# Sample attention of a hybrid decoder: four pages of values in four column groups, and scores of two sequences to a step

## The chip, the cores and the metric

The kernel runs on one NeuronCore of a Trainium2 chip. Its engines are TensorE (matmuls; PE in the rows, its weight loads PEld), VectorE (DVE), ScalarE (ACT), GpSimd (POOL) and SyncE (SP), each with an instruction queue of its own that it works off in order; 16 DMA engines move data between HBM and SBUF. The metric is the device time of one execution in microseconds (us); the time of a kernel is the median of its runs.

## The reference

One inference step of a two-layer decoder, for a prompt of 512 tokens and a group of 8 samples with one new token each. Each layer is a half-step FFN, a mixer and a half-step FFN. The first layer's mixer joins differential attention (4 heads, two softmax maps each) with gated linear attention (GLA); the second's is an mLSTM. The change lies in the attention of the 8 samples, over 2048 cached keys and values each, in 16 pages of 128 positions that a page table points to:

```python
def diff_weights(logits, lam):
    p = jax.nn.softmax(logits, axis=-1)
    return p[:, :, 0] - lam * p[:, :, 1]

def diff_attn_sample(q, k_new, v_new, k_past, v_past, lam, slopes):
    ...
    logits = jnp.concatenate([
        alibi_logits(q, k_past, q_pos, jnp.arange(past), slopes),
        alibi_logits(q, k_new, q_pos, q_pos, slopes)], axis=-1)
    w = diff_weights(logits, lam)
    return (jnp.einsum('bhqk,bkhv->bqhv', w[..., :past], v_past.astype(F32))
            + jnp.einsum('bhqk,bkhv->bqhv', w[..., past:], v_new.astype(F32)))
...
        k_past = cache_k[e, page_table].reshape(dec_b, past, H_A, 2, DK_A)
        v_past = cache_v[e, page_table].reshape(dec_b, past, H_A, DV_A)
        a_out = diff_attn_sample(aq, ak, av, k_past, v_past, lam, slopes)
```

The new token attends to the past and to itself; per sequence, head and map there is one row of 2048 scores, and per sequence and head one row of 128 values comes out. Everything is fp32.

## The kernel before

The program is one straight row of stages: FFN, the even mixer (`even`), two FFNs, the odd mixer, FFN. Dense products are split into a high and a low half (fp32r operands; three matmuls at lines 100 to 102), and their weights come through `raw`, which in the even mixer is fetched over GpSimd's queue.

The even mixer computes, in this order, queries and keys of the prompt (tiles `pj`, the projections), values, prompt attention (`aps`, `atp`, `ao`), then GLA for two pairs of heads (`gla_pair`: masked products `glv`, decays `gdc`, state updates `gu`, outputs `go`; `gla_sample`: `gsu`, `gso`), then the output projection (`project`, tile `y`). Four more projections (`gates`, tile `pj`) are dealt out over the first GLA pair; the second has none.

The attention of the samples is a generator, `sample_steps`, that is advanced between other work: `tick(us)` adds the time of the work just written down and advances the queue by one step for each `rate` (1.65 us) of it; the projection's `rest` empties what is left (`tick(1e9)`). The generator writes:

- Scores (line 730, tile `sps`). A unit is two pages of keys (512 KB, `kv_unit`, two DMAs from SP's queue, four buffers of tile `kv`). For each of 8 groups `u` of two pages and each of 8 sequences `b`, four matmuls, one per head, with 32 stationary columns in column group `h` (`tile_position=(0, 32 * h)`), stream 256 key positions. One sequence to a step.
- Softmax over [128 rows = 4 heads x 32, 2048] (`sc`, `sm`, `m1`), and 16 transposes (`stp`) that turn the weights so that positions lie on partitions.
- Values (line 776, tile `so`). For each `b`, each group `g` of four pages and each page `i`, four matmuls, one per head in its column group, stream the 128 value columns of that head. The stationary `pw` is zero but for the two columns of the sequence (line 771 copies them in, line 768 clears the old ones on GpSimd, after the matmuls that read them). One unit of two pages to a step, 8 matmuls.
- The end (lines 783 to 790): scale by `w`, one matmul with `sel` that turns and sums the rows, one for the new token, and two adds into `oa`.

Instructions are not run in the order in which the code writes them. A scheduler puts them on each engine's queue by priority (work within `tc.high_priority` first) and by when its model of the machine has their operands ready; so a step's matmuls can be apart on TensorE, with other matmuls between them. An fp32 matmul shows as two passes in the profile (each a weight load and a matmul), a transpose and an fp32r matmul as one.

Of the kernel before, what the change touches and what calls it, by code (L numbers as in the profile page):

```python
# [7 lines left out]
F32 = mybir.dt.float32  # L8
# [3 lines left out]
ALU = mybir.AluOpType  # L12
# [3 lines left out]
P = 128  # L16
# [3 lines left out]
NS = 8  # L20
# [9 lines left out]
KU, PTU, KVB, PLAG = 2, 2, 4, 8  # L30
# [25 lines left out]
class Net:  # L56
# [663 lines left out]
    def sample_steps(self):  # L720

        nc, ev = self.nc, self.ev
        mx = self.smx
        sc = []
        for u in range(16 // KU):
            ps = self.plong.tile([P, 512], F32, tag="long", name="sps")
            for b in range(NS):
                kt = self.kv_unit(self.t["ckt"], "kt")
                for h in range(4):
                    nc.tensor.matmul(ps[32 * h:32 * h + 32, :KU * P], lhsT=self.q2[:, b, h, :],  # L730
                                     rhs=kt[:, :, h * P:h * P + P], start=(b == 0), stop=(b == NS - 1),
                                     tile_position=(0, 32 * h))
                if b < NS - 1:
                    yield True
            if u % 2 == 0:
                sc.append(ev.tile([P, 512], F32, tag="sc", name="sc", bufs=SCB))
            r = slice(KU * P * (u % 2), KU * P * (u % 2 + 1))
            nc.vector.tensor_tensor_reduce(out=sc[-1][:, r], in0=ps[:, :KU * P], in1=self.sbias[:, r], scale=1.0,
                                           scalar=-3e38, op0=ALU.add, op1=ALU.max, accum_out=mx[:, u:u + 1])
            yield True  # L740
        sm, nb, m1 = [ev.tile([P, 9], F32, tag=f"sm{i}", name="ssm") for i in range(3)]
        off = self.sbias[:, 512:521]
        nc.vector.tensor_tensor(out=nb, in0=mx, in1=off, op=ALU.add)
        nc.vector.tensor_reduce(out=m1[:, 0:1], in_=nb, axis=AX.X, op=ALU.max)
        nc.vector.tensor_scalar(nb, off, m1[:, 0:1], None, ALU.subtract)
        for g in range(4):
            nc.scalar.activation(sc[g], sc[g], AF.Exp, bias=nb[:, 2 * g:2 * g + 1], accum_out=sm[:, g:g + 1])
        nc.scalar.activation(sm[:, 4:5], mx[:, 8:9], AF.Exp, bias=nb[:, 8:9])
        nc.vector.tensor_reduce(out=m1[:, 1:2], in_=sm[:, :5], axis=AX.X, op=ALU.add)
        nc.vector.reciprocal(m1[:, 2:3], m1[:, 1:2])  # L750
        w = m1[:, 3:4]
        nc.vector.tensor_tensor(out=w, in0=self.rw, in1=m1[:, 2:3], op=ALU.mult)
        nc.vector.tensor_tensor(out=self.wnew, in0=sm[:, 4:5], in1=w, op=ALU.mult)
        yield True
        tps = []
        for g in range(4):
            tp = self.bank("stp")
            for i in range(4):
                nc.tensor.transpose(tp[:, i * P:i * P + P], sc[g][:, i * P:i * P + P], self.ident)
            s = ev.tile([P, 512], F32, tag="sc", name="spt", bufs=SCB)  # L760
            self.evict(s, tp)
            tps.append(s.rearrange("p (i h x) -> p i h x", i=4, h=4))
            yield True
        o = self.plong.tile([P, 512], F32, tag="long", name="so")
        for b in range(NS):
            if b:
                for a in self.pw:
                    nc.gpsimd.memset(a[:, :, :, 2 * b - 2:2 * b], 0.0)
            for g in range(4):
                pw = self.pw[g % 2]  # L770
                nc.vector.tensor_copy(pw[:, :, :, 2 * b:2 * b + 2], tps[g][:, :, :, 2 * b:2 * b + 2])
                for i in range(4):
                    if i % KU == 0:
                        vt = self.kv_unit(self.t["cv"], "vtile")
                    for h in range(4):
                        nc.tensor.matmul(o[32 * h:32 * h + 32, :P], lhsT=pw[:, i, h, :],  # L776
                                         rhs=vt[:, i % KU, h * P:h * P + P], start=(b == 0 and g == 0 and i == 0),
                                         stop=(b == NS - 1 and g == 3 and i == 3), tile_position=(0, 32 * h))
                    if i % KU == KU - 1 and not (b == NS - 1 and g == 3 and i == 3):
                        yield True  # L780

        ob = self.vtile()[:, :P]
        nc.vector.tensor_scalar(ob, o[:, :P], w, None, ALU.mult)
        yield True
        f = self.bank("sf")
        nc.tensor.matmul(f[:, :32], lhsT=ob, rhs=self.sel, start=True, stop=True)
        nc.tensor.matmul(f[:, 32:64], lhsT=self.wnew.to_broadcast([P, P]), rhs=self.sel, start=True, stop=True)
        z = self.oa[:, :, SEQ:]
        nc.vector.tensor_tensor(out=z, in0=f[:, 32:64].rearrange("p (h b) -> p h b", h=4), in1=self.vs, op=ALU.mult)
        nc.vector.tensor_tensor(out=z, in0=f[:, :32].rearrange("p (h b) -> p h b", h=4), in1=z, op=ALU.add)  # L790

    def attn_weights(self, i, h):
        nc, at = self.nc, self.at
# [237 lines left out]
    def even(self, w_in, w_out):  # L1031
        from contextlib import ExitStack
        nc, tc, t = self.nc, self.tc, self.t
        with ExitStack() as ctx:
# [3 lines left out]
            def const(name, shape, dt=F32, pool=None):  # L1038
                a = (pool or ev).tile(shape, dt, tag=name, name=name)
                nc.gpsimd.dma_start(out=a, in_=t[name])  # L1040
                return a
# [8 lines left out]
            bhn = const("bhn", [P, 4])  # L1050
            self.sbias = const("sbias", [P, 521])
            self.sel = const("sel", [P, 32])
            rm = const("rmask", [P, 2])
            lt = ev.tile([P, 2], F32, tag="lt", name="lt")
            self.nlam = ev.tile([P, 1], F32, tag="nlam", name="nlam")
# [16 lines left out]
            self.vs = ev.tile([P, 4, NS], F32, tag="vs", name="vs")  # L1072
            self.qs = ev.tile([P, 4, NS], F32, tag="qs", name="qs")
            oa = self.oa = ev.tile([P, 4, T], F32, tag="oa", name="oa")
            self.pw = [ev.tile([P, 4, 4, 32], F32, tag=f"pw{i}", name="pw") for i in range(2)]
            self.q2 = ev.tile([P, NS, 4, 32], F32, tag="q2", name="q2")
            for a in self.pw + [self.q2]:
                nc.gpsimd.memset(a, 0.0)
# [19 lines left out]
            with ExitStack() as c2:  # L1098
# [60 lines left out]
                ob = self.ob = gl.tile([P, 4, T], F32, tag="ob", name="ob")  # L1159
# [536 lines left out]
def even_consts():  # L1696
    f = np.float32
    c = {}
    p = np.arange(P)
    half, sel, rm = np.zeros((P, 32), f), np.zeros((P, 32), f), np.zeros((P, 2), f)  # L1700
    half[:64, 0], half[64:, 1] = 1, 1
    slope = SLOPE
    sb = np.zeros((P, 521), f)
    for h, b, m in itertools.product(range(4), range(NS), range(2)):
            r = 32 * h + 2 * b + m
            sb[r, :512] = [-slope[h] * (512 - c_) for c_ in range(512)]
            sb[r, 512:520] = [-slope[h] * (2048 - 512 * (g // 2 + 1)) for g in range(8)]
            rm[r, m] = 1
            sel[r, 8 * h + b] = 1
    c["half"], c["sbias"], c["rmask"], c["sel"] = half, sb, rm, sel  # L1710
    dist = 384 + p[:, None] - np.arange(512)[None, :]
    c["dist"] = np.where(dist >= 0, -dist, -1e30).astype(f)
    lvl = np.zeros((P, 9, P), f)
    msk = np.zeros((P, 8, P), np.int32)
    a, b = p[:, None], p[None, :]
    for lv in range(7):
        w = 64 >> lv
        mid = b // (2 * w) * (2 * w) + w
        lvl[:, lv, :] = np.where(b >= mid, (a >= mid) & (a <= b), (a > b) & (a < mid)) / 16.0
        msk[:, lv, :] = (a // (2 * w) == b // (2 * w)) & (a % (2 * w) < w) & (b % (2 * w) >= w)  # L1720
    lvl[:, 7, :] = (a <= b) / 16.0
    lvl[:, 8, :] = (a > b) / 16.0
    msk[:, 7, :] = a == b
    c["lvl"], c["gmask"] = lvl.reshape(P, 9 * P), msk
    return c
# [119 lines left out]
```

## Time and profile before

| | before |
|---|---|
| median of 3 runs | 2262.44 us (2254.84 to 2271.28) |
| the profiled execution | 2272.11 us, its span 2270.3 us |
| TensorE busy | 2224.2 us (98%), 18340 matmuls |
| VectorE, ScalarE, GpSimd busy | 1513.6 (67%), 1010.9 (45%), 47.5 us (2%) |
| mean granted clock of TensorE | 0.977 |
| HBM read, written | 276.22 MB, 17.11 MB |
| `kt<-ckt`, `vtile<-cv` | 128 issues each, 256 KB each, 4.3 and 3.7 us to landing |

A row of the profile names line, engine, operation, and tiles as out<-in, with the operand's partitions x elements; busy times are those that the profiler records, so in a pipelined row of matmuls the recorded ends overlap the next start, and the distance from start to start is what a matmul takes. The granted clock is the share of 2.4 GHz that TensorE's throttle let through (1.00 or 0.50; other figures are means over a stretch). The even mixer lies between about 340 and 835 us, the sample scores between 428 and 584, the sample values between 596 and 801.

### The profile page before, as it was taken

To read this page: it belongs to the slowest core of one execution; us is meant where nothing else is said; L and a number is where in the kernel's file an instruction comes from. 1 tells how busy PE (TensorE), PEld (TensorE's weight loads), DVE (VectorE), ACT (ScalarE), POOL (GpSimd) and SP (SyncE) were. 2 spreads that over 40 slices of the span, in tenths; PEclk is the share of its full clock that TensorE was granted. 3 is DMA by queue.
4 is the path that set the end of the run, shared out by engine and by line. 5 is a ranking of instruction groups with operands and counts; after the bars stand their busy time and mean duration, and the time that the engine had idled before them with its cause. 6 is when DMAs were issued, how large, how long until landed. Compare 5 with 4: busy or idle time off the path is not lost.

```text
span 2270.3 us, 45692 instructions
## 1 busy us (share of the span) xinstructions
PE 2224.2 (98%) x18340; PEld 2082.8 (92%) x18340; DVE 1513.6 (67%) x3161; ACT 1010.9 (45%) x1932; POOL 47.5 (2%) x112
## 2 busy tenths in 40 slices
PE   8999999999999999999999999999999999999999
PEld 8999998776776689999999999999889899999999
DVE  8858586435664478676768758586745588858683
ACT  6535354335522255344444535353545555525352
POOL 0000001000000000000000000000000000000000
PEclk9999999999996699999999999999999999999999
DMA  5324234587775552323223324232554464233322
GB/s 179 110 66 133 67 111 134 177 275 249 246 233 168 169 186 66 121 85 112 84 85 112 112 67 129 73 102 75 140 154 145 149 205 141 93 103 94 103 84 85
DMA packets 107019, 296.30 MB, mean 131 GB/s; under 512 B 12129, under 2 KB 16786, under 8 KB 106678
## 3 DMA queue, kind: packets, MB, share of 16 engines
q1 hardware_dynamic: 93504, 254.91, 35.3%
q0 software_dynamic: 7536, 25.42, 3.6%
q10 hardware_dynamic: 5766, 13.05, 1.6%
q8 instruction: 144, 2.36, 0.4%
q14 instruction: 69, 0.57, 0.1%
HBM read 276.22 MB, written 17.11 MB: 129 GB/s over the span
## 4 chain that ended last, share of the span: by engine, by line
PE 84%; DVE 6%; DMA 6%; ACT 2%; issue 2%; SPq 0%; POOL 0%; ACTq 0%; POOLq 0%; DVEq 0%
PE y L100 9%; PE y L101 8%; PE y L102 8%; PE A L100 6%; PE A L101 6%; PE A L102 6%; PE pj L100 3%; PE pj L101 3%; PE pj L102 3%; PE E L101 3%; PE E L100 3%; PE E L102 3%; DMA cs<-sc 2%; PE glv L899 2%; PE so L776 2%
## 5 line engine op out<-in xcount | busy, mean ns | idle before, releaser
L105 ACT CAST whi<-raw 128x512 fp32r<-128x512 f32 (+1 forms) x440 | 351.2, 806 | 435.0 <-PE y L101 171.3
L106 DVE TENSOR_TENSOR wlo<-raw,whi 128x512 fp32r<-128x512 f32 (+1 forms) x440 | 402.0, 922 | 156.4 <-ACT whi L105 142.5
L100 PE MATMUL y<-hh,whi 128*128 128x256 f32 (+1 forms) x1408 | 398.1, 283 | 0.0
L101 PE MATMUL y<-hl,whi 128*128 128x256 f32 (+1 forms) x1408 | 397.9, 283 | 0.0
L102 PE MATMUL y<-hh,wlo 128*128 128x256 f32 (+1 forms) x1408 | 396.8, 282 | 0.0
L100 PE MATMUL pj<-xh,whi 128*128 128x264 f32 (+1 forms) x896 | 263.8, 295 | 16.1 <-ACT gs L1531 3.2
L101 PEld LDWEIGHTS y<-hl,whi 128*128 128x128 f32 x1408 | 265.1, 188 | 1.0 <-DVE hl L106 0.6
L100 PEld LDWEIGHTS y<-hh,whi 128*128 128x128 f32 x1408 | 264.7, 188 | 0.8
L102 PEld LDWEIGHTS y<-hh,wlo 128*128 128x128 f32 x1408 | 264.8, 188 | 0.0
L102 PE MATMUL pj<-xh,wlo 128*128 128x264 f32 (+1 forms) x896 | 257.4, 288 | 2.9 <-DVE wlo L106 2.9
L101 PE MATMUL pj<-xl,whi 128*128 128x264 f32 (+1 forms) x896 | 258.6, 289 | 0.0
L100 PE MATMUL A<-xb,whi 128*128 128x264 f32 (+1 forms) x864 | 249.3, 290 | 0.7
L101 PE MATMUL A<-xb,whi 128*128 128x264 f32 (+1 forms) x864 | 244.2, 284 | 0.0
L102 PE MATMUL A<-xb,wlo 128*128 128x264 f32 (+1 forms) x864 | 243.0, 284 | 0.1
L105 ACT CAST whi<-graw 128x1024 fp32r<-128x1024 f32 x144 | 147.6, 1049 | 162.5 <-PE y L101 103.9
L100 PEld LDWEIGHTS pj<-xh,whi 128*128 128x128 f32 x896 | 173.1, 193 | 33.1 <-issue 10.3
L549 DVE SCALAR_TENSOR_TENSOR x<-y,x 128x256 f32<-128x256 f32 (+1 forms) x192 | 81.9, 427 | 180.5 <-PE y L102 180.1
L106 DVE TENSOR_TENSOR wlo<-graw,whi 128x1024 fp32r<-128x1024 f32 x144 | 172.6, 1219 | 30.9 <-ACT whi L105 30.9
L102 PEld LDWEIGHTS pj<-xh,wlo 128*128 128x128 f32 x896 | 172.9, 193 | 5.0 <-DVE wlo L106 3.3
L101 PEld LDWEIGHTS pj<-xl,whi 128*128 128x128 f32 x896 | 173.2, 193 | 4.0 <-issue 3.5
L100 PEld LDWEIGHTS A<-xb,whi 128*128 128x128 f32 x864 | 162.5, 188 | 9.2 <-DVE c L476 2.6
L100 PE MATMUL E<-xh,whi 128*128 128x264 f32 x576 | 163.7, 284 | 1.6 <-ACT whi L105 1.6
(468 smaller groups left out, 5179.9 us busy)
## 6 DMA issues: line engine op xcount, KB each, us to landing
raw<-w SPq DMA_DIRECT2D x240, 512.0 KB, 3.6
graw<-w SPq DMA_DIRECT2D x72, 512.0 KB, 4.4
kt<-ckt SPq DMA_DIRECT2D x128, 256.0 KB, 4.3
vtile<-cv SPq DMA_DIRECT2D x128, 256.0 KB, 3.7
raw<-w POOLq DMA_DIRECT2D x40, 512.0 KB, 4.5
cs<-sc SPq DMA_DIRECT2D x16, 512.0 KB, 6.9
kb<-kqd SPq DMA_DIRECT2D x16, 512.0 KB, 6.9
o_cs<-cs ACTq DMA_DIRECT2D x16, 512.0 KB, 5.3
```

Of the source, the lines that this page charges most:

```text
L100: nc.tensor.matmul(ps, lhsT=wh, rhs=xh, start=(ends[0] and i == ks[0]), stop=False, skip_group_check=open_)
L101: nc.tensor.matmul(ps, lhsT=wh, rhs=xl, start=False, stop=False, skip_group_check=open_)
L102: nc.tensor.matmul(ps, lhsT=wl, rhs=xh, start=False, stop=(ends[1] and i == ks[-1]), skip_group_check=open_)
L105: self.nc.scalar.copy(out=hi, in_=src)
L106: self.nc.vector.tensor_tensor(out=lo, in0=src, in1=hi, op=ALU.subtract)
L549: nc.vector.scalar_tensor_tensor(xs, y[:, :n], -0.5, xs, ALU.mult, ALU.add)
L776: nc.tensor.matmul(o[32 * h:32 * h + 32, :P], lhsT=pw[:, i, h, :], rhs=vt[:, i % KU, h * P:h * P + P], start=(b == 0 and g == 0 and i == 0 ...
L899: nc.tensor.matmul(ps[:, j * P:j * P + P], lhsT=lhs[r, j * P:j * P + P], rhs=rhs[r, j * P:j * P + P], start=True, stop=True)
```

## The change

Scores: the step takes two sequences. The first unit of keys is requested, a step ends, the second is requested, and then come the eight matmuls of both. The number of steps is the same.

Values: the roles are turned. The four pages `i` of a group now go to the four column groups, and each matmul streams the whole row of 512 values (four heads of 128). The 32 stationary columns hold four sequences x 4 heads x 2 maps (`pw` is [128, 4, 32]), so the work runs in two halves `hf` of four sequences each, each with its own `so` bank; per sequence and group of pages there are four matmuls after both units were requested, 128 in all. Rows of `so` mean page group, sequence, head and map, so that the weight per row is brought into that order by two matmuls with `perm` (`sw`, `wr`), and each half ends with a scaling of 512 columns and four matmuls with `sel2` (`sf`, `fs`) that sum over the page groups.

```diff
-            for b in range(NS):
-                kt = self.kv_unit(self.t["ckt"], "kt")
-                for h in range(4):
-                    nc.tensor.matmul(ps[32 * h:32 * h + 32, :KU * P], lhsT=self.q2[:, b, h, :],
-                                     rhs=kt[:, :, h * P:h * P + P], start=(b == 0), stop=(b == NS - 1),
-                                     tile_position=(0, 32 * h))
-                if b < NS - 1:
+            for b in range(0, NS, 2):
+                kts = [self.kv_unit(self.t["ckt"], "kt")]
+                yield True
+                kts.append(self.kv_unit(self.t["ckt"], "kt"))
+                for i, kt in enumerate(kts):
+                    for h in range(4):
+                        nc.tensor.matmul(ps[32 * h:32 * h + 32, :KU * P], lhsT=self.q2[:, b + i, h, :],
+                                         rhs=kt[:, :, h * P:h * P + P], start=(b + i == 0), stop=(b + i == NS - 1),
+                                         tile_position=(0, 32 * h))
+                if b < NS - 2:
                     yield True
...
+        f = self.bank("sw")
+        for hf in range(2):
+            nc.tensor.matmul(f[:, hf:hf + 1], lhsT=self.perm[:, hf * P:hf * P + P], rhs=w, start=True, stop=True)
+        wr = ev.tile([P, 2], F32, tag="wr", name="wr")
+        fs = ev.tile([P, 4, NS], F32, tag="fs", name="fs")
+        nc.vector.tensor_copy(wr, f[:, :2])
...
-        o = self.plong.tile([P, 512], F32, tag="long", name="so")
-        for b in range(NS):
-            if b:
-                for a in self.pw:
-                    nc.gpsimd.memset(a[:, :, :, 2 * b - 2:2 * b], 0.0)
-            for g in range(4):
-                pw = self.pw[g % 2]
-                nc.vector.tensor_copy(pw[:, :, :, 2 * b:2 * b + 2], tps[g][:, :, :, 2 * b:2 * b + 2])
-                for i in range(4):
-                    if i % KU == 0:
-                        vt = self.kv_unit(self.t["cv"], "vtile")
-                    for h in range(4):
-                        nc.tensor.matmul(o[32 * h:32 * h + 32, :P], lhsT=pw[:, i, h, :],
-                                         rhs=vt[:, i % KU, h * P:h * P + P], start=(b == 0 and g == 0 and i == 0),
-                                         stop=(b == NS - 1 and g == 3 and i == 3), tile_position=(0, 32 * h))
-                    if i % KU == KU - 1 and not (b == NS - 1 and g == 3 and i == 3):
+        for hf in range(2):
+            o = self.plong.tile([P, 512], F32, tag="long", name="so")
+            for b in range(4):
+                if hf or b:
+                    old = slice(8 * ((b + 3) % 4), 8 * ((b + 3) % 4) + 8)
+                    for a in self.pw:
+                        nc.gpsimd.memset(a[:, :, old], 0.0)
+                for g in range(4):
+                    pw = self.pw[g % 2]
+                    x = 8 * hf + 2 * b
+                    nc.vector.tensor_copy(pw[:, :, 8 * b:8 * b + 8].rearrange("p i (h m) -> p i h m", h=4),
+                                          tps[g][:, :, :, x:x + 2])
+                    vts = [self.kv_unit(self.t["cv"], "vtile")]
+                    yield True
+                    vts.append(self.kv_unit(self.t["cv"], "vtile"))
+                    for i in range(4):
+                        nc.tensor.matmul(o[32 * i:32 * i + 32, :], lhsT=pw[:, i, :], rhs=vts[i // KU][:, i % KU, :],
+                                         start=(b == 0 and g == 0), stop=(b == 3 and g == 3), tile_position=(0, 32 * i))
+                    if b < 3 or g < 3:
                         yield True
...
+            ob = self.vtile()[:, :512]
+            nc.vector.tensor_scalar(ob, o, wr[:, hf:hf + 1], None, ALU.mult)
+            yield True
+            f = self.bank("sf")
+            for h in range(4):
+                nc.tensor.matmul(f[:, 4 * h:4 * h + 4], lhsT=ob[:, h * P:h * P + P], rhs=self.sel2[:, 4 * h:4 * h + 4],
+                                 start=True, stop=True)
+            nc.vector.tensor_copy(fs[:, :, 4 * hf:4 * hf + 4], f[:, :16].rearrange("p (h b) -> p h b", h=4))
...
-            self.pw = [ev.tile([P, 4, 4, 32], F32, tag=f"pw{i}", name="pw") for i in range(2)]
+            self.pw = [ev.tile([P, 4, 32], F32, tag=f"pw{i}", name="pw") for i in range(2)]
```

The left-out lines load the two new constants (`sel2`, `perm`) and add `fs` into `oa`.

The order of instructions on the engines follows. Its rows give line, operation, tiles, and shape of the output; "x4" is four alike in a row. The first place is TensorE's queue in the second GLA pair, at its first state update `gsu`; `so` is the sample values, `glv`, `gso`, `gsu` and `gsot` belong to GLA. Before:

```order
L776 MATMUL so<-vtile,pw 32x128 x8
L1011 MATMUL gsu<-vt,ks 64x512 x2
L899 MATMUL glv<-gkq 128x128 x4
L776 MATMUL so<-vtile,pw 32x128 x8
L1021 MATMUL gso<-gst,qm 32x128 x4
L899 MATMUL glv<-gkq 128x128 x4
L776 MATMUL so<-vtile,pw 32x128 x8
L1027 MATMUL gsot<-ident,vt 128x128
```

The same place on TensorE's queue after the change:

```order
L917 MATMUL glv<-gkq 128x128 x4
L1029 MATMUL gsu<-vt,ks 64x512
L790 MATMUL so<-vtile,pw 32x512 x2
L1029 MATMUL gsu<-vt,ks 64x512
L917 MATMUL glv<-gkq 128x128 x3
L790 MATMUL so<-vtile,pw 32x512
L917 MATMUL glv<-gkq 128x128
L1039 MATMUL gso<-gst,qm 32x128 x3
L917 MATMUL glv<-gkq 128x128
L790 MATMUL so<-vtile,pw 32x512
```

Before, the eight matmuls of a step stood together; now the four of a step stand apart, as two, one and one, with GLA's matmuls between them, which are themselves cut.

The second place is TensorE's queue in the output projection, in the last steps of the sample values; `y` is the projection, `hst` and `hs` the statistics of a norm. Before:

```order
L224 MATMUL hst<-ident,row 128x128
L776 MATMUL so<-vtile,pw 32x128 x4
L224 MATMUL hst<-ident,row 128x128 x2
L101 MATMUL y<-xl,whi 128x256
L102 MATMUL y<-xh,wlo 128x256
L776 MATMUL so<-vtile,pw 32x128 x4
L100 MATMUL y<-xh,whi 128x256
```

The same place on TensorE's queue after the change:

```order
L102 MATMUL y<-xh,wlo 128x256
L790 MATMUL so<-vtile,pw 32x512 x2
L214 MATMUL hs<-sq,one 32x256
L790 MATMUL so<-vtile,pw 32x512
L224 MATMUL hst<-ident,row 128x128 x2
L100 MATMUL y<-xh,whi 128x256
L101 MATMUL y<-xl,whi 128x256
L102 MATMUL y<-xh,wlo 128x256
L100 MATMUL y<-xh,whi 128x256
L790 MATMUL so<-vtile,pw 32x512
```

Here too a group of four column groups was whole before; now it is three entries of the row. In the whole program `so` stands in 84 runs on TensorE before (36 of four matmuls, 25 of eight, 15 longer or of five to nine, 8 of fewer than four), and in 77 after (46 of one, 17 of two, 8 of three, 6 of four); `sps` in 51 before and 42 after.

## Rows read from the trace of the kernel before

**Rows 1.** The page, parts 1, 2 and 4: busy time, granted clock, chain.

```profile
PE 2224.2 (98%) x18340; PEld 2082.8 (92%) x18340; DVE 1513.6 (67%) x3161; ACT 1010.9 (45%) x1932; POOL 47.5 (2%) x112
...
PEclk9999999999996699999999999999999999999999
...
PE 84%; DVE 6%; DMA 6%; ACT 2%; issue 2%; SPq 0%; POOL 0%; ACTq 0%; POOLq 0%; DVEq 0%
```

**Rows 2.** Busy by stretch: length, PE, PEld, DVE, ACT, POOL; clock, DMA share, GB/s.

```profile
428.00:596.00 168.00, 165.31 (x1476) 119.77 (x1474) 75.90 (x279) 73.38 (x182) 10.33 (x20) 1.00 0.77 256
596.00:701.00 105.00, 104.59 (x1217) 81.56 (x1216) 68.35 (x165) 32.71 (x89) 7.34 (x23) 0.98 0.75 246
702.00:776.00 74.00, 74.00 (x441) 47.49 (x433) 24.37 (x73) 9.31 (x24) 1.85 (x6) 0.50 0.39 125
```

**Rows 3.** The same stretches, matmuls and weight loads of tile `so` alone.

```profile
596.00:701.00 105.00, 28.53 (x640) 16.50 (x640) 0.00 (x0) 0.98 0.75 246
702.00:776.00 74.00, 20.25 (x236) 7.00 (x228) 0.00 (x0) 0.50 0.39 125
776.00:802.00 26.00, 7.17 (x152) 3.08 (x144) 0.34 (x1) 1.00 0.84 282
```

**Rows 4.** What TensorE waited for, 428 to 802: total us, times, longest.

```profile
PE sps L730 <- DMA kt<-ckt: 1.3, 2, 0.8
PE so L776 <- DMA vtile<-cv: 0.5, 1, 0.5
```

**Rows 5.** Timeline of TensorE at full clock (start us, recorded us, matmul, count).

```profile
664.89 0.64 PE L776 MATMUL so<-vtile,pw 128*32 128x128 f32 x16
665.47 1.16 PE L899 MATMUL glv<-gkq 64*128 64x128 f32 x8
...
692.09 0.41 PE L776 MATMUL so<-vtile,pw 128*32 128x128 f32 x2
692.43 1.09 PE L934 MATMUL gu<-bv,gkn 128*64 128x128 f32 x16
...
785.25 0.28 PE L101 MATMUL y<-xl,whi 128*128 128x256 f32 x1
785.37 0.28 PE L102 MATMUL y<-xh,wlo 128*128 128x256 f32 x1
785.58 0.43 PE L776 MATMUL so<-vtile,pw 128*32 128x128 f32 x8
785.93 0.39 PE L101 MATMUL y<-xl,whi 128*128 128x256 f32 x1
```

**Rows 6.** The same view: a 512-wide fp32 matmul at full clock, and its follower.

```profile
640.22 1.07 PE L1011 MATMUL gsu<-vt,ks 8*64 8x512 f32 x2
641.22 0.64 PE L776 MATMUL so<-vtile,pw 128*32 128x128 f32 x14
```

**Rows 7.** The same view at half clock.

```profile
708.96 1.96 PE L1011 MATMUL gsu<-vt,ks 8*64 8x512 f32 x2
710.85 0.66 PE L776 MATMUL so<-vtile,pw 128*32 128x128 f32 x8
711.44 1.96 PE L1011 MATMUL gsu<-vt,ks 8*64 8x512 f32 x2
...
750.11 0.41 PE L101 MATMUL y<-xl,whi 128*128 128x256 f32 x1
750.32 0.41 PE L102 MATMUL y<-xh,wlo 128*128 128x256 f32 x1
```

**Rows 8.** Busy time by stretch: a short spell at half clock.

```profile
640.00:643.00 3.00, 3.00 (x26) 1.06 (x21) 1.42 (x6) 0.00 (x0) 0.00 (x0) 1.00 0.71 211
643.00:647.00 4.00, 4.00 (x20) 3.72 (x20) 2.09 (x13) 0.00 (x0) 0.00 (x0) 0.57 0.73 254
```

**Rows 9.** Tile `kt`: from issue to landing.

```profile
DMA to landing us min/median/max: 2.6/4.3/8.2
```

**Rows 10.** What GpSimd waited for: total us, times, longest.

```profile
POOL pw L768 <- PE so L776: 112.6, 13, 29.3
```

More of the change, by code (lines that the diff above doesn't have):

```diff
@@ L782, in sample_steps @@
-        ob = self.vtile()[:, :P]
-        nc.vector.tensor_scalar(ob, o[:, :P], w, None, ALU.mult)
-        yield True
+        for hf in range(2):
[17 more added lines that the diff above has]
+                    if b < 3 or g < 3:
+                        yield True
+            ob = self.vtile()[:, :512]
[6 more added lines that the diff above has]
+            nc.vector.tensor_copy(fs[:, :, 4 * hf:4 * hf + 4], f[:, :16].rearrange("p (h b) -> p h b", h=4))
@@ L785, in sample_steps @@
         f = self.bank("sf")
-        nc.tensor.matmul(f[:, :32], lhsT=ob, rhs=self.sel, start=True, stop=True)
-        nc.tensor.matmul(f[:, 32:64], lhsT=self.wnew.to_broadcast([P, P]), rhs=self.sel, start=True, stop=True)
+        nc.tensor.matmul(f[:, :32], lhsT=self.wnew.to_broadcast([P, P]), rhs=self.sel, start=True, stop=True)
         z = self.oa[:, :, SEQ:]
-        nc.vector.tensor_tensor(out=z, in0=f[:, 32:64].rearrange("p (h b) -> p h b", h=4), in1=self.vs, op=ALU.mult)
-        nc.vector.tensor_tensor(out=z, in0=f[:, :32].rearrange("p (h b) -> p h b", h=4), in1=z, op=ALU.add)
+        nc.vector.tensor_tensor(out=z, in0=f[:, :32].rearrange("p (h b) -> p h b", h=4), in1=self.vs, op=ALU.mult)
@@ L792, in attn_weights @@
+        nc.vector.tensor_tensor(out=z, in0=fs, in1=z, op=ALU.add)
     def attn_weights(self, i, h):
@@ L1052, in even @@
             self.sel = const("sel", [P, 32])
+            self.sel2 = const("sel2", [P, 16])
+            self.perm = const("perm", [P, 2 * P])
             rm = const("rmask", [P, 2])
@@ L1709, in even_consts @@
             sel[r, 8 * h + b] = 1
+    sel2, perm = np.zeros((P, 16), f), np.zeros((P, 2 * P), f)
+    for i, b, h, m in itertools.product(range(4), range(NS), range(4), range(2)):
+        r = 32 * i + 8 * (b % 4) + 2 * h + m
+        sel2[r, 4 * h + b % 4] = 1
+        perm[32 * h + 2 * b + m, b // 4 * P + r] = 1
+    c["sel2"], c["perm"] = sel2, perm
     c["half"], c["sbias"], c["rmask"], c["sel"] = half, sb, rm, sel
```

## The prediction

> **What bounds the kernel now.** The page comes first: TensorE is recorded busy for 2224.2 of 2270.3 us, and 84% of the chain that ended last runs over it [rows 1]. A saving or a cost on TensorE is therefore one of the whole kernel, as long as other engines keep up. The sample scores (tile `sps`) and values (tile `so`) are fed, step by step, into other work between 428 and 802 us, so the busy time of those stretches comes next: TensorE works 165.31 of 168, 104.59 of 105 and 74.00 of 74 us there, VectorE and ScalarE well under half to two thirds [rows 2]. In that whole time TensorE waited 1.3 us for pages of keys and 0.5 us for pages of values [rows 4]. Neither transfers nor VectorE bound this part; the length of the instruction row on TensorE does.
>
> Two things in it price the change. First, the row of the granted clock dips in two slices [rows 1]: from 702 to 776 us the clock was 0.50, that is 1.2 of 2.4 GHz, though TensorE is recorded busy all the time [rows 2]. What it did there is the second GLA pair: masked 64-row products, the 8-row `gsu`, and pieces of `so`, all fp32, with no dense projection between them. A short dip of the same kind stands at 643 to 647 us, clock 0.57 [rows 8], behind a `gsu`. Second, `so` alone is recorded for 28.53, 20.25 and 7.17 us in the three stretches, 55.95 us together [rows 3]. Recorded ends overlap the next start by some 0.07 us a piece (16 passes: 0.64 recorded, 0.58 from start to next start [rows 5]); over 84 pieces in TensorE's order that is 6 us, so `so` really takes about **50 us**.
>
> **The price of a piece.** A "piece" is a run of `so` matmuls with nothing else between. An fp32 matmul shows as two passes. One matmul alone (2 passes) takes 692.43 - 692.09 = 0.34 us; four matmuls on four column groups (8 passes) take 785.93 - 785.58 = 0.35 us; sixteen passes take 0.58 us [rows 5]. So four that stand side by side cost what one costs: they run at once, and one that stands alone pays the whole price for a quarter of the work. For 512 columns the nearest row is `gsu`, one fp32 matmul of 512 columns that does not fill the array: two passes take 641.22 - 640.22 = 1.00 us at full clock [rows 6] and 710.85 - 708.96 = 1.89 us at half; a piece of 8 passes of 128 columns takes 0.59 us at half [rows 7].
>
> **What the change does to the row.** It removes 512 matmuls of 128 columns and adds 128 of 512. The streamed columns stay the same, 65,536. If the four pages of a step ran as one piece, 32 pieces would do. They do not: TensorE's order after the change has 77 pieces, 46 of one matmul, 17 of two, 8 of three and only 6 of four. Before, only 8 of the 84 held fewer than four. A 128-wide group of four was short enough to be placed whole between two pieces of other work; the four 512-wide ones are dealt out one by one, as the two excerpts of the order show.
>
> Counted by place: 37 pieces stand ahead of the first `gsu` of the second GLA pair (where the clock fell), 22 from there to the pair's last `go`, 18 after that among the dense `y` of the output projection. With the clock low over the same work as now: 37 x 1.00 + 22 x 1.89 + 18 x 1.00 = 96.6 us, against 50: **+47 us**.
>
> The smaller parts. Scores: the same 256 matmuls in 42 pieces instead of 51; a joined piece saves 2 x 0.35 - 0.58 = 0.12 us [rows 5], nine of them **-1 us**. The two passes with `perm`, eight small ones with `sel2` instead of one, and a second read-out of 512 columns: no row shows them alone; below, nothing (other matmuls stand behind each read-out), above, three more switches and two short waits, 2 us; I take **+1 us**. Transfers: bytes and issues are the same, but two units of 512 KB now come free together and are wanted together. A pair is used every 2 x 168/64 = 5.2 us, two pairs are in flight, so each has some 9 us to land; a unit takes 4.3 us in the median, 8.2 at most [rows 9], and two that share the engines twice the median, 8.6. I take nothing; the cover is gone if they take 10, and then each of 32 pairs of keys costs about 1 us. GpSimd clears the old columns of `pw` after `so` has read them, and waited 112.6 us for it in 13 waits [rows 10]; weight fetches of the projection are queued behind these clears. They move later with `so`. I take nothing, since so does everything that wants these weights; at worst two fetches come late, under 10 us.
>
> **The clock.** The longer the stretch of fp32 pieces, the later the dense `y` rows get the clock back, and now a `so` of one column group stands after every 6 to 17 of them. The row shows the clock up again at 776 us. I expect the low level to last about halfway through the 18 last pieces: 9 x 0.89 = 8 us, and half of the 148 `y` matmuls there at 0.21 instead of 0.12 us [rows 5, 7], 7 us: **+15 us**. In the first pair, where the clock dipped once for some 3.4 us (643 to 647 us at a mean of 0.57 [rows 8]), single pieces make more such spells; two or three more cost half their length each: **+4 us**.
>
> Sum: 47 - 1 + 1 + 15 + 4 = **+66 us**. The profiled execution took 2272.11 us, 2270.3 of it the span; the median of the runs is 2262.44. Against the execution that is 2338, against the median **2328 us**.
>
> **Where a rule says otherwise.** The row gives a single instruction almost no price: 8 passes cost 0.01 us more than 2 [rows 5], so having 768 passes fewer is worth nothing by itself. The Trainium skill, TensorEngine Tiling (Array Packing), section Instruction Overhead, holds some 60 cycles for each matmul; as an estimate at 2.4 GHz that would be 25 ns x 768 = 19 us of gain, and the sum by it +47 instead of +66. The trace does not agree where four tiles run at once.
>
> **The rivals.** (1) *The four pages do run side by side*, because TensorE has the next ones ready. Then 32 pieces, 7 of them in the low stretch: 25 x 1.00 + 7 x 1.89 = 38 us, 12 us less than now: about 2250 us, not slower. For it: the pages land in time [rows 4], so nothing but the order keeps the four apart. Against it: the order itself, and the 0.34 us of a lone matmul [rows 5]. It decides if the 512-wide pieces number fewer than about 45.
> (2) *The clock stays up*, because TensorE streams long matmuls without a break. Then all 77 pieces cost 77 us, 27 more, and the other work of the low stretch (74 us less 29.5 pieces x 0.59 = 17 for `so`, so 57) takes half, 28 less: about 2261 us, the same as before. Against it: the clock fell in the row while the engine was recorded busy without a gap [rows 2], behind just such fp32 pieces, of which there are now more in a row. The Trainium skill, TensorE: Matmul & The Clock Gate, Part 1, has the gate open with a busy engine and close with an idle one, which would favour this rival. By that, 74.00 busy of 74 us at 0.50 should not be there; the trace disagrees.
> (3) *The clock stays low from the first pair on, to the last value*: then another 9 pieces and 74 `y` (16 us), and in the first pair most of 28 pieces x 0.89 and of some 50 us of other work: about +60 more, 2390 us.
> (1) and (2) together would give 32 - 50 - 28 = -46, about 2216 us; that is the one way to a clear gain.
>
> **How the numbers follow.** Forecast, 0.78: slower, 2328, own range 2289 to 2360. Low end: all pieces at full price, other work as now, +27. High end: all 40 pieces from the second pair on, and all 148 `y`, at half clock (+47 + 16 + 14 = 77) and a third of the first pair low (8 of pieces, 12 of the rest): +97. Rival (1) 0.05, (2) 0.06, (3) 0.08, both of (1) and (2) 0.03. The range is the forecast's own, which leaves out about 2 in 10. About 1%, 23 us, is what a measurement of this kernel tells from no change. Slower by more: 0.86 (forecast and (3)). Within: 0.11. Faster: 0.03.
>
> **What would show it.** Right: `so` with 256 passes in some 77 pieces, about 1.0 us each at full clock and 1.9 at half, 90 to 110 us together; a longer low stretch from about 700 us, ending among the `y` of the projection; the stretch before 590 us unchanged. Wrong: `so` near 40 us together; lone 512-wide pieces at 0.3 us; a clock row without dips; or TensorE idle in front of `sps` for `kt`, or of `y` for weights that wait behind the clears.

## The result, and the profile after

The change made the kernel slower: 2283.47 us in the median of ten runs (2276.22 to 2290.47), beside 2255.14 for the kernel before in as many (2239.38 to 2271.28). The ratio is 1.0125, interval 1.0091 to 1.0159. So it cost 28 us, less than half of the 66 forecast, and the median lies below the range. Ratios, here and below, leave out runs more than 1.5% above the fastest of their kernel; medians and the table count them. The profiled execution took 2289.14 us (span 2287.4), 17.0 more than the one profiled before.

The page after, parts 1, 2 and 4, as in [rows 1]:

```profile
PE 2238.1 (98%) x17590; PEld 2058.3 (90%) x17590; DVE 1516.1 (66%) x3165; ACT 1010.1 (44%) x1932; POOL 48.1 (2%) x114
...
PEclk9999999999998999999999999999999999999999
...
PE 85%; DVE 6%; DMA 4%; ACT 3%; issue 2%; SPq 0%; ACTq 0%; DVEq 0%; POOLq 0%
```

TensorE is the bound as before, and the low slices of the clock row (6 and 6) have become a single 8. Busy time by stretch, columns as in [rows 2]; the last row is the longest spell at half clock:

```profile
428.00:596.00 168.00, 164.71 (x1480) 121.87 (x1479) 73.99 (x271) 69.85 (x173) 10.70 (x20) 1.00 0.78 260
596.00:701.00 105.00, 105.00 (x667) 64.92 (x666) 64.19 (x161) 30.62 (x81) 6.20 (x19) 0.98 0.66 215
702.00:776.00 74.00, 73.94 (x345) 36.95 (x341) 32.58 (x92) 12.94 (x38) 1.64 (x6) 0.88 0.45 142
718.50:735.60 17.10, 17.10 (x46) 7.63 (x45) 5.26 (x13) 0.90 (x2) 0.12 (x1) 0.50 0.30 92
```

From 702 to 776 us the clock was 0.50 before and is 0.88 now: the low level (1.2 GHz) lasts 17 us there, not 74. Tile `so` alone, as in [rows 3], and its matmuls by the view of the tile (count, then min/median/max ns of a pass):

```profile
596.00:701.00 105.00, 35.83 (x136) 4.94 (x136) 0.75 (x1) 0.98 0.66 215
702.00:776.00 74.00, 30.29 (x70) 3.67 (x66) 0.00 (x0) 0.88 0.45 142
776.00:820.00 44.00, 18.99 (x51) 2.61 (x50) 0.15 (x1) 1.00 0.70 231
```
```profile
L790 PE MATMUL so<-vtile,pw x256: 592/617/1062, 598.7 to 819.2; 128*32 128x512 f32 x128
...
  DMA vtile<-cv: 1.0, 2
...
  POOL pw L780: 84.6, 11
```

85.1 us are recorded; from start to next start, summed over the trace, `so` takes 78.9 us (70.7 of it at full clock, 10 of the 256 passes at half), where it took 49.7 before. Pages made TensorE, weight loads included, wait 1.0 us, and GpSimd waited 84.6 us for `so`, less than in [rows 10].

The same row in time, TensorE around the second pair's first `gsu` (columns as in [rows 5]):

```profile
710.17 1.06 PE L790 MATMUL so<-vtile,pw 128*32 128x512 f32 x6
711.16 0.22 PE L1008 MATMUL gst<-ident,gs 8*128 8x8 f32 x1
...
712.22 1.04 PE L790 MATMUL so<-vtile,pw 128*32 128x512 f32 x2
713.20 0.39 PE L932 MATMUL gdc<-lvl,gh 128*128 128x256 f32 x1
...
716.69 1.07 PE L1029 MATMUL gsu<-vt,ks 8*64 8x512 f32 x2
717.69 0.93 PE L917 MATMUL glv<-gkq 64*128 64x128 f32 x6
718.55 1.92 PE L790 MATMUL so<-vtile,pw 128*32 128x512 f32 x2
720.40 0.79 PE L917 MATMUL glv<-gkq 64*128 64x128 f32 x2
...
735.11 1.29 PE L1029 MATMUL gsu<-vt,ks 8*64 8x512 f32 x2
736.32 1.04 PE L790 MATMUL so<-vtile,pw 128*32 128x512 f32 x2
```

Three matmuls (6 passes) start 0.99 us before the next entry, one (2 passes) 0.98: a lone 512-wide one pays the price of three side by side. At half clock it pays 1.85. The clock falls behind `gsu` and `glv`, at 718.5 us, as it did before at 701, but is back at 735.6 us, while single pieces of `so` stand in the row.

### The profile page after: what moved, and what is told of

The parts are those of the page before. It is cut to its first block, busy times and chain, and to the rows that moved or that the text cites. A ratio compares the mean times of both kernels' runs of the same rounds, so it can differ in the third digit from the quotient of the medians.

```text
span 2287.4 us, 44198 instructions
## 1 busy us (share of the span) xinstructions
PE 2238.1 (98%) x17590; PEld 2058.3 (90%) x17590; DVE 1516.1 (66%) x3165; ACT 1010.1 (44%) x1932; POOL 48.1 (2%) x114
## 4 chain that ended last, share of the span: by engine, by line
PE 85%; DVE 6%; DMA 4%; ACT 3%; issue 2%; SPq 0%; ACTq 0%; DVEq 0%; POOLq 0%
PE y L100 8%; PE y L101 8%; PE y L102 8%; PE A L100 6%; PE A L101 6%; PE A L102 6%; PE pj L100 4%; PE pj L101 4%; PE pj L102 3%; PE so L790 3%; PE E L101 3%; PE E L100 3%; PE E L102 3%; DMA cs<-sc 2%; PE glv L917 2%
```

## The experiments

The expectations speak of three theories. P: the price of a piece. C: the clock falls behind the 8-row `gsu` among 64-row products, and long streams over all 128 rows bring it back. F, the prediction's: more fp32 pieces in a row keep it low longer. "Clock" is the mean granted clock of a whole run; `so` is summed from start to next start in the profiled execution (for the kernel before, that of [rows 1]). The kernel before stood beside each group of runs (1 to 4, 5 to 7, 9 to 11), with medians of 2256.21, 2255.73 and 2257.59 us.

The time of a run goes with its clock. A straight line through these 59 runs of before gives 2227.7 us at a clock of 1 and 1.9 us more for each .001 below it; the runs scatter about it by 2 us. The last column says how far the runs of a kernel lie from that line in the mean: what the kernel costs or saves at an equal clock, an estimate good to some 2 us.

| kernel | runs | median us | lowest (clock) | highest (clock) | `so` us | us at equal clock |
|---|---|---|---|---|---|---|
| before (beside 5 to 7) | 19 | 2255.73 | 2234.12 (.996) | 2272.93 (.977) | 49.7 | 0 |
| the change | 10 | 2283.47 | 2276.22 (.995) | 2290.47 (.990) | 78.9 | +40.0 |
| 1 four together | 10 | 2242.97 | 2233.85 (.994) | 2260.36 (.981) | 34.0 | -5.5 |
| 2 before, `gsu` of 128 rows | 4 | 2241.89 | 2240.76 (.992) | 2242.87 (.991) | 44.8 | -2.4 |
| 3 both of these | 9 | 2246.3 | 2240.85 (.993) | 2255.98 (.986) | 33.9 | +0.5 |
| 4 values alone | 4 | 2286.23 | 2279.34 (.994) | 2290.56 (.989) | 79.1 | +41.8 |
| 5 change, `gsu` of 128 rows | 4 | 2272.45 | 2270.36 (.995) | 2273.91 (.992) | 73.0 | +31.8 |
| 6 scores alone | 10 | 2255.96 | 2233.17 (.995) | 2269.46 (.977) | 42.1 | -1.1 |
| 7 values twice | 10 | 2258.91 | 2251.07 (.997) | 2265.37 (.992) | 67.7 | +19.0 |
| 9 `gsu` twice | 10 | 2261.67 | 2240.86 (.992) | 2274.66 (.973) | 42.9 | -2.2 |
| 10 as 1, five units | 10 | 2255.27 | 2233.14 (.992) | 2263.75 (.980) | 35.0 | -5.6 |
| 11 as 3, five units | 6 | 2237.95 | 2231.22 (.994) | 2243.52 (.989) | 32.9 | -5.4 |

(One execution of 3, at 4197 us, is left out. Number 8, as 1 with five units and nothing given up for them, gave no time: its last pool wants 27.5 KB of SBUF per partition, and 25.3 KB are left.)

So at an equal clock the change costs 40 us: at .995 its runs took 2276.22 to 2277.52 us, those of before 2234.45 to 2238.06. It costs 28 by the medians because its clock is higher, .989 to .995 with a median of .9915, where the 59 runs of before go from .977 to .996 with a median of .984. The clock gave some 12 us back.

**The two halves of the change.** Experiment 4 takes the scores' part back, experiment 6 does it alone.

```diff
-            for b in range(NS):
-                kt = self.kv_unit(self.t["ckt"], "kt")
+            for b in range(0, NS, 2):
+                kts = [self.kv_unit(self.t["ckt"], "kt")]
+                yield True
+                kts.append(self.kv_unit(self.t["ckt"], "kt"))
...
```

> The change without its scores part: one sequence to a step as before, values as after. Theory P: everything comes from the values; `so` in 77 pieces, 77 to 82 us, and the time 20 to 36 us over the kernel before, as with the whole change. A rival, that the paired loads of keys cost part of it: 10 us or more below the whole change.

> The scores' part of the change alone, two sequences to a step: 42 pieces of `sps` in place of 51. P: nine switches fewer at 0.12 us each, -1 us: 2254 to 2257 us, the stretch before 590 us 0 to 2 us shorter, and the dip of the clock in the second GLA pair as before. If the scores carry a part of the loss (transfers of two units that are wanted together): 2262 us or more, and TensorE waits for `kt` for more than 5 us in front of `sps`.

Values alone gave ratio 1.0103 (1.0064 to 1.0142), scores alone 1.0027 (0.998 to 1.0073). The loss is the values'; the scores' part can't be told from nothing. The higher clock comes with the values too: .989 to .994 in experiment 4, .977 to .995 in experiment 6.

Experiment 6 also shows how loosely the clock hangs on the row. Its TensorE row here is the one of before, without a fall:

```profile
698.30 0.65 PE L779 MATMUL so<-vtile,pw 128*32 128x128 f32 x16
698.88 1.07 PE L1014 MATMUL gsu<-vt,ks 8*64 8x512 f32 x4
699.88 1.16 PE L902 MATMUL glv<-gkq 64*128 64x128 f32 x8
700.97 0.64 PE L779 MATMUL so<-vtile,pw 128*32 128x128 f32 x16
```

The kernel before, the same four entries:

```profile
698.69 0.64 PE L776 MATMUL so<-vtile,pw 128*32 128x128 f32 x16
699.26 1.07 PE L1011 MATMUL gsu<-vt,ks 8*64 8x512 f32 x4
700.27 1.32 PE L899 MATMUL glv<-gkq 64*128 64x128 f32 x8
701.51 1.08 PE L776 MATMUL so<-vtile,pw 128*32 128x128 f32 x16
```

From `glv` on this one runs at half clock, for 75 us; the other profile has no spell there, and took 2233.17 us. So these entries of the row don't fix the spell, and its length differs from execution to execution. The runs of before go from 2234 us at clock .996 to 2273 at .977, and the profiled one, at .977, is at the low end: 47 of the 59 have .988 or less, so some low stretch is the rule, but the median run, at .984, has by this measure some two thirds of the profiled one's.

**The four matmuls kept together.** Experiment 1 lets the fourth matmul, whose page comes last, be placed first, and puts the others behind it.

```diff
+                    with self.tc.high_priority(400):
+                        last = product(3)
+                        with self.tc.issue_after(last.ins):
+                            for i in range(3):
+                                product(i)
```

> The changed kernel, with the four value matmuls of a step kept together on TensorE (31 pieces of `so` instead of 77). Theory P (a piece of 512-wide matmuls costs about 1.0 us at full clock, whether it holds one matmul or four): `so` takes 31 to 36 us instead of 79, and the time falls by up to 46 us from the 2283 of the change. A rival, that the pages of values arrive too slowly and set the pace, has `so` wait: time within 10 us of the change. On the clock, theory C (the fall is set off by the 8-row `gsu` among 64-row products, and long unbroken 128-row matmuls bring the clock back) has a long low stretch again, 40 to 75 us, and a time of 2240 to 2262. Theory F (the more fp32 pieces in a row, the longer the clock stays low; that of the prediction) has it no longer than the 17 us of the change, and about 2237.

The ratio is 0.9941 (0.991 to 0.9973), 40 us less than the change. `so` fell to 34.0 us in 31 pieces, as by P, and four side by side take 1.00 us (615.06 - 614.06, below). At an equal clock the two kernels lie 45 us apart (+40.0 and -5.5), near P's 46; by the medians it is less because this one's clock is lower (median .988). What TensorE waited for most from 588 to 865 us, the two stretches, and the longest spell at half clock:

```profile
PE so L790 <- DMA vtile<-cv: 7.7, 6, 2.4
```
```profile
596.00:701.00 105.00, 98.39 (x736) 69.94 (x734) 69.60 (x173) 35.12 (x92) 7.64 (x22) 0.95 0.71 235
702.00:776.00 74.00, 70.46 (x435) 45.88 (x432) 41.15 (x128) 19.86 (x48) 3.92 (x11) 0.86 0.68 227
711.00:728.10 17.10, 17.10 (x74) 10.44 (x72) 6.55 (x20) 2.56 (x7) 0.00 (x0) 0.50 0.42 137
```

TensorE stands idle for 6.6 of 105 us where the change had it busy for all 105, and the clock is 0.95 there. On the theories of the clock the run is split: its longest spell is 17.1 us, as F had it and not the 40 to 75 of C, but its time is in C's range and 6 us above F's 2237. One of the shorter dips stands behind a wait:

```profile
611.41 0.28 PE L100 MATMUL pj<-xh,whi 128*128 128x264 f32 x1
614.06 1.06 PE L790 MATMUL so<-vtile,pw 128*32 128x512 f32 x8 [2.37 <-DMA vtile<-cv]
615.06 0.39 PE L101 MATMUL pj<-xl,whi 128*128 128x264 f32 x1
615.28 0.29 PE L102 MATMUL pj<-xh,wlo 128*128 128x264 f32 x1
615.40 0.39 PE L100 MATMUL pj<-xh,whi 128*128 128x264 f32 x1
615.59 0.42 PE L101 MATMUL pj<-xl,whi 128*128 128x264 f32 x1
```

**`gsu` over 128 rows.** Experiment 2 is the kernel before, with the state update's operands filled up with zeros, experiment 3 adds this to experiment 1, and experiment 5 to the change.

```diff
-        ks = gl.tile([NS, P], F32, tag="ks", name="ks")
+        ks = gl.tile([P, P], F32, tag="ks", name="ks")
+        nc.vector.memset(ks, 0.0)
...
-                vd = self.vtile()[:NS, :SEQ].rearrange("p (b v) -> p b v", b=4)
+                vd = self.vtile()[:, :SEQ]
+                nc.vector.memset(vd, 0.0)
...
```

> The kernel before, with the state update `gsu` of the samples' GLA fed over 128 rows, zero but for the 8, instead of over 8 rows; its width and passes are the same. Theory C: the low stretch of some 75 us in the second GLA pair does not come, the 57 us of other work in it run at double speed, and the time falls by 25 to 37 us, to 2218 to 2230. Theory F: the fp32 pieces are the same, so the low stretch is still 60 to 75 us and the time within 8 us of the kernel before.

> Both edits on the changed kernel: four value matmuls together, and `gsu` over 128 rows. Theories P and C: `so` 31 to 33 us, no low stretch in either GLA pair: 17 us less for `so` than before and 28 to 37 less for the clock, 2200 to 2212 us. Theory F: as the run with the four together alone, within 5 us.

> The whole change, and GLA's state update `gsu` over 128 rows (zeros in 120 of them), as in the second experiment. It pins the clock, so that against the second experiment only the price of the pieces is left. P (price: each of some 75 pieces about 1.0 us at full clock, against 41 us for the shorter ones): `so` 75 to 80 us, 2242 + 36 to 40 = 2276 to 2284 us. C (the clock falls behind the 8-row `gsu` among 64-row products, and long unbroken streams bring it back): no spell over 10 us at half clock between 690 and 780 us. F (fp32 pieces of `so` in a row keep the clock low): a spell of 15 us or more there, `so` 85 us or more, 2285 us or more.

Experiment 2, the second pair (timeline, and the stretches):

```profile
706.55 0.64 PE L776 MATMUL so<-vtile,pw 128*32 128x128 f32 x16
707.13 1.08 PE L1013 MATMUL gsu<-vt,ks 128*64 128x512 f32 x4
708.14 1.16 PE L899 MATMUL glv<-gkq 64*128 64x128 f32 x8
709.22 0.64 PE L776 MATMUL so<-vtile,pw 128*32 128x128 f32 x16
```
```profile
702.00:776.00 74.00, 72.98 (x792) 51.65 (x790) 44.68 (x135) 21.71 (x53) 4.38 (x13) 1.00 0.71 233
669.30:683.00 13.70, 13.70 (x99) 11.78 (x99) 4.89 (x10) 1.62 (x4) 0.13 (x1) 0.50 0.72 236
```

Two `gsu` of 128 rows take 1.01 us (708.14 - 707.13), as those of 8 rows did, and the clock stays at 1.00 where it was 0.50. One profile without the spell is no proof, since experiment 6 has one too; the runs are: all four have a clock of .990 to .992. The ratio is 0.9918 (0.9887 to 0.9949), a gain of 14 us, under the 25 to 37 expected: they were counted from the one execution with 75 low us, and there is a new spell, from 669.3 us, right behind a wait of 1.34 us for a page:

```profile
668.68 0.43 PE L776 MATMUL so<-vtile,pw 128*32 128x128 f32 x8 [1.34 <-DMA vtile<-cv]
669.03 2.84 PE L899 MATMUL glv<-gkq 64*128 64x128 f32 x16
```

Experiment 3 missed its 2200 to 2212: ratio 0.9966 (0.9925 to 1.0007). TensorE works only 94.75 of 105 us from 596 on:

```profile
596.00:701.00 105.00, 94.75 (x682) 65.63 (x681) 66.80 (x169) 32.68 (x87) 6.87 (x20) 0.95 0.66 220
```

Experiment 5 measures P at nearly the clock of experiment 2 (.992 to .995 and .990 to .992); the change's stretch from 702 us, now:

```profile
702.00:776.00 74.00, 73.39 (x395) 38.14 (x395) 36.40 (x111) 14.64 (x40) 3.49 (x11) 1.00 0.53 167
```

No spell is left in the pair. Against experiment 2, with the same `gsu`, the change costs 2272.45 - 2241.89 = 31 us, and 34 at an equal clock; against experiment 6's profile, which has no spell there either, `so` takes 73.0 instead of 42.1 us. P's 36 to 40 was somewhat high; F's spell is not there. Against the change itself, 2283.47 - 2272.45 = 11 us came off, but 8 of them at an equal clock (+40.0 to +31.8), so only some 3 by the clock; where the 8 come from was not sought.

**Work that is only added.** In experiment 7 each group of value matmuls of the kernel before is issued twice, in experiment 9 each 8-row `gsu`. The order on TensorE moves with it: counted in the traces, `so` stands in 70 and 72 pieces, before in 92.

```diff
+                    for j in range(2):
+                        for h in range(4):
+                            nc.tensor.matmul(o[32 * h:32 * h + 32, :P], lhsT=pw[:, i, h, :],
...
```
```diff
-                nc.tensor.matmul(ps[64 * i:64 * i + 64, :], lhsT=ks[:, 64 * i:64 * i + 64],
-                                 rhs=vd, start=True, stop=True)
+                for j in range(2):
+                    nc.tensor.matmul(ps[64 * i:64 * i + 64, :], lhsT=ks[:, 64 * i:64 * i + 64],
+                                     rhs=vd, start=j == 0, stop=j == 1)
```

> The kernel before, with each group of four value matmuls issued twice in a row (the values come out doubled): work is only added, in longer streams over all 128 rows. Price: 128 groups more at 0.58 - 0.35 = 0.23 us is +29 us at full clock, +36 us with half of the second GLA pair's at half clock. C (streams over all rows bring the clock back): the spell at half clock in the second GLA pair is under 25 us, and the time 2256 + 29 - 10 to - 25 = 2260 to 2275 us. F (fp32 pieces keep the clock low): the spell is 60 us or longer, and the time 2290 us or more.

> The kernel before, with each 8-row `gsu` of GLA's state update issued twice, in one accumulation (the two GLA layers' states of the samples take in twice the new term): 8 matmuls of 1.0 us more. Work is only added, as with the values issued twice, but over 8 rows instead of 128. Price alone: +8 us at full clock, less some 2 us for 67 instead of 84 pieces of `so`: 2260 to 2265 us, with the clock as before. C (8-row matmuls among 64-row products bring the clock down): a spell of 40 us or longer in the second GLA pair, also spells of 10 us or more in the first, and 2270 to 2300 us. F (fp32 pieces of `so` in a row keep the clock low): these pieces are as before, so as by price, with half of the added work at half clock, 2264 to 2270 us.

Experiment 7 is the sharpest of the set. F wanted 2290 us or more; it took 2258.91, ratio 1.0032 (0.9997 to 1.0068): `so` grew to 67.7 us, and the kernel did not get measurably slower. Its clock over ten runs is .991 to .997 (median .994). The profiled stretches, with no low spell in either pair:

```profile
596.00:701.00 105.00, 104.97 (x1636) 87.21 (x1635) 63.52 (x148) 29.07 (x75) 7.37 (x21) 1.00 0.67 223
702.00:776.00 74.00, 72.96 (x1151) 58.97 (x1150) 40.63 (x120) 18.81 (x51) 3.39 (x11) 1.00 0.69 222
```

The pieces of `so` are fp32 and hold twice the matmuls, and the clock is higher. This is the opposite of what the prediction had them do. The added work is not free: at the lowest run of each it costs 2251.07 - 2234.12 = 17 us, over all runs 19 at an equal clock, less than the 29 counted; the higher clock gave nearly all of it back.

Experiment 9 went C's way weakly. Clocks of .973 to .992, a lowest run at a lower clock than before's, but a ratio of 1.0009 (0.9965 to 1.0054), and in the profile the long spell is 17 us, where C wanted 40:

```profile
706.50:723.60 17.10, 17.10 (x116) 11.22 (x116) 7.31 (x20) 1.81 (x5) 0.00 (x0) 0.50 0.31 112
```

It doesn't separate the theories.

**Five units of pages.** Experiments 10 and 11 are 1 and 3 with one buffer more for the pages; for the room there is one score buffer fewer, and `perm` is fetched into a temporary.

```diff
-KU, PTU, KVB, PLAG = 2, 2, 4, 8
+KU, PTU, KVB, PLAG = 2, 2, 5, 8
...
-SCB, APB = 5, 5
+SCB, APB = 4, 5
...
+        perm = self.vtile()[:, :2 * P]
+        nc.gpsimd.dma_start(out=perm, in_=self.t["perm"])
...
```

> The first experiment (the four value matmuls of a step kept together) with five buffers for units of two pages instead of four; the room comes from one score buffer fewer and from `perm`, which is fetched into a temporary. If the missing gain of the first experiment is the wait of `so` for pages (13.3 us in ten waits): these are under 4 us in all, no spell over 10 us at half clock stands behind such a wait, and the time is 2225 to 2236 us. If it is the work that the early values push back (`pj` 34 instead of 25 us): `pj` stays at 32 us or more, and the time is 2240 to 2246 us.

> The same with `gsu` over 128 rows. If waits were what kept the third experiment at 2247 us: 2222 to 2234 us, and no spell over 7 us at half clock between 600 and 800 us. If the pieces of four, being shorter together, leave the 64-row products in longer runs of their own, with the clock down behind them: spells of 10 us or more in the two GLA pairs without a wait ahead of them, and 2240 to 2250 us.

By the view of tile `so`, the pages still cost 6.4 us in experiment 10, half of the 13.3 in experiment 1, yet the median rose to 2255.27 (ratio 0.9984, 0.9948 to 1.0019). The profile has a low spell of 37 us with no wait ahead of it, but an 8-row `gsu`:

```profile
695.10 1.07 PE L1037 MATMUL gsu<-vt,ks 8*64 8x512 f32 x2
696.10 1.16 PE L925 MATMUL glv<-gkq 64*128 64x128 f32 x8
...
698.69 0.63 PE L1047 MATMUL gso<-gst,qm 128*32 128x128 f32 x2
699.26 1.22 PE L925 MATMUL glv<-gkq 64*128 64x128 f32 x4
```
```profile
698.70:736.20 37.50, 37.50 (x152) 23.61 (x152) 14.98 (x44) 5.40 (x16) 0.84 (x3) 0.50 0.44 150
```

Neither forecast holds: `pj` is back at 27 us, and the clock (median .9835) took the gain; at an equal clock it lies where experiment 1 does, -5.6 us. With `gsu` over 128 rows as well, experiment 11 reached 2237.95 us, ratio 0.9913 (0.9881 to 0.9945), between its two forecasts. It is the best median here, 46 us under the change's, but can't be told from experiment 2, which leaves the values as they were before.

## Why the prediction was right in direction and wrong in size

**Right: the count and the price of the pieces.** 77 pieces at about 1.0 us were forecast; the 70.7 us at full clock are of 246 passes, and a piece takes 0.98 us by the rows above. Experiment 1 shows the cause by taking it away: with 31 pieces `so` costs 34.0 us, and the kernel is 40 us faster than the change. Rival (1), four side by side at 2250 us, is thereby seen as it would have been. In the sum the pieces at full clock make 77 less 42.1 (`so` without a spell, experiment 6), 35 us; at an equal clock the change costs 40.

**Right, or too small to tell: scores, transfers, clears.** Experiment 6 gives nothing for the scores. TensorE waited 1.0 us for values' pages. Weights behind the clears of `pw` show little: TensorE's `y` waited 2.2 us for `xh` and 1.0 for `wlo`, and the `y` up to the first matmul of the FFN that follows are 61.4 us instead of 55.6; how much of that 5.8 is the clears' was not tried.

**Wrong: the clock, in three terms.** The price of 22 pieces at 1.89 us, the +15 for a longer low level and the +4 for more dips all rest on one step: "the longer the stretch of fp32 pieces, the later the dense `y` rows get the clock back". Some 31 of the 66 us are this; the runs show some 12 the other way. After the change the low level in the second pair lasted 17 us, not past 776, and the first pair has one dip of the old length (its clock 0.98 as before), not two or three more. So `so` came to 78.9 us, not to 104.6 (96.6, and the 8 us of pieces in the +15): 26 us. The other work between the first `so` and the first matmul of the FFN that follows shrank from 191.7 us (241.4 less 49.7) to 181.1 (260.0 less 78.9), 11 less, where +12 was forecast: 22 us (`glv` 45.8 to 37.4, `go` 15.4 to 11.4). Together 48 of the 49 us between +66 and the +17 from profile to profile. Rival (2) had the sign of the clock right, but priced it as gone altogether.

The step also rests on a wrong reading. The stretch from 702 to 776 us is not without a dense projection: [rows 7] have `y` at 750 us, behind which the clock stayed at 0.50 for some 25 us more. (And in rival (3) nine pieces and 74 `y` are 15 us by its rows, not 16; nothing hangs on it.)

Experiment 7 shows the step false: more fp32 value matmuls, in longer pieces over all 128 rows, and the clock is higher. What the low spell does depend on, experiments 2, 3, 5 and 11 show: filling `gsu` from 8 to 128 rows, at the same 1.01 us, raised the median clock each time against the same kernel without it (.984 to .9915, .988 to .991, .9915 to .993, .9835 to .9915). The twelve profiles agree. Between 596 and 802 us the clock fell 21 times in them. Twelve of the falls stand behind or in waits of TensorE, of 0.8 to 4.0 us together. The other nine have no idle time in the row just ahead of them, and each has an 8-row `gsu` in the 4 us before it; none of the nine is in a profile whose `gsu` has 128 rows. Such a `gsu` does not bring a fall each time: experiments 6 and 7 have none behind theirs. What decides that, and what in the values' part raised the clock of the change (the 512-wide matmuls, by likeness with experiment 7, or the new order of the row), stays open.

**Wrong beneath it: one execution taken for the kernel.** Half of the forecast's terms were priced with [rows 2 and 3], from an execution with 75 us at half clock. The three times then known (2254.84 to 2271.28) spread by 16 us, and the profiled one was at their top. Of the 59 runs of before with a clock on record, 12 have .991 or more and take 2234 to 2248 us, and only two have a clock as low as the profiled one's; a change's cost had to be worked out at both levels.

The Trainium skill, TensorE: Matmul & The Clock Gate, Part 1, ties the gate to how busy the engine is. The traces agree for the falls behind a wait (experiment 1 at 615 us, experiment 2 at 669), but not for the nine in a row without a gap (701 us before, 718 after the change, 699 in experiment 10).

## What to carry to other kernels

Price matmuls in column groups by pieces as they stand in the engine's order, not by columns: four side by side cost what a lone one costs (1.0 us for 512 fp32 columns here), and a scheduler that can deal them out singly may do so, as here. Read a low clock in one profile together with the spread of the run times before counting on it, and work out the change at both levels. Where each run's clock is on record, compare kernels at an equal clock as well as by their medians. If low stretches stand behind matmuls of few rows, try filling these up with zeros: it cost nothing in matmul time here, and the kernel before became 14 us faster, nearly all of it by the clock.

## What was not expected of the hardware

Added matmul work can pay for itself: 512 more value matmuls cost 19 us at an equal clock, but moved the median by 3 us, since no run's clock then fell under .991. And a TensorE recorded busy without a gap was granted half its clock or the whole of it behind the same four entries of the row, in the kernel before and in experiment 6, with 1.08 or 0.64 us for the same 16 passes.
